# Dense expert weights built once per token over all 128 first keys, with one-hots laid out by pairs of tokens and a contiguous stationary operand

## Chip, cores and metric

One core of a Trainium2 chip runs the whole program. The metric is device time in microseconds (us), median over runs. The engines named below are PE (matrix multiply; PEld is its weight load), DVE (vector), ACT (scalar), POOL and SP (in this part only issuers of DMAs). Every engine runs its own instructions in program order and waits on semaphores for the others.

## What is computed

The program is two transformer layers of different kinds; the change lies in the feed-forward part of the first, a product-key mixture with 16,384 tiny experts (`peer_ffn`), for 256 tokens:

```python
q = (h @ w_q).reshape(b, s, PEER_HEADS, 2, PEER_HALF)
sc = jnp.einsum('bshpc,hpkc->bshpk', q, sub_keys)
top_v, top_i = lax.top_k(sc, PEER_TOPK)                # 16 of 128 keys, twice per head
cand_i = top_i[..., 0, :, None] * PEER_KEYS + top_i[..., 1, None, :]
best_v, best_pos = lax.top_k(cand_v, PEER_TOPK)        # 16 of 256 pairs per head
idx = jnp.take_along_axis(cand_i, best_pos, axis=-1)   # 8 heads x 16 experts per token
gate = jax.nn.softmax(best_v, axis=-1)
act = jax.nn.gelu(jnp.einsum('chkd,cd->chk', u_tab[idx], h))
out = jnp.einsum('chk,chkd->cd', gate * act, v_tab[idx])
```

An expert's number is (first key) x 128 + (second key). The reference gathers 128 experts per token; the kernel computes all 16,384 densely.

## The kernel before

The experts are a 128 x 128 grid: second key on the partitions, first key along the free axis. `act[0]` and `act[1]` are two tiles of 128 partitions x 64 first keys x 256 tokens (f32), one for each half of the first keys. Three kinds of work make the part:

- `u_phase(half)` (L1245) computes gelu(U h) for one half. It goes by pairs of first keys. A pair is one PSUM tile `pa` of 512 columns, and each of its two keys needs one 512 KB item of the weight stream and 24 matmuls of 256 columns (the weights are split into a high and a low part, and three products are added). It yields after the first key and after the second, so 64 steps in all. ACT applies the gelu from PSUM into `act[half]` (L1253).
- `g_phase(half)` (L1274) makes the dense routing weights G of one half and multiplies them into `act[half]`. It goes by groups of 8 tokens, 32 groups. `prep` makes on DVE three things in f16: `b`, the one-hot of the first keys (64 keys x 8 tokens, L1279); `a`, the one-hot of the second keys (128 x 8, L1281); and `c`, which is `b` times the gate in a high and a low part (two multiplies, L1283). The partition here is the token's 128 chosen experts. For each of the 8 tokens two matmuls follow, stationary `a[:, :, i]` and moving `c[:, q, :, i]` of 64 columns, both with neighbouring elements 8 halves apart. A DVE instruction (L1297) multiplies the PSUM tile into `act[half]`. A group is two steps, `prep` of the next group and the matmuls.
- `v_phase(half)` (L1314) multiplies the result with the V table: per first key one stream item and 12 matmuls of 512 columns, accumulated over both halves in four PSUM banks (`vacc`, tiles `pb`). Per two keys `split_to` (L386) splits `act` into a high part on ACT and a low part on DVE.

Order and overlap are written out by hand: `weave(main, (side, rate))` (L268) takes `rate` steps of the side generator after each step of the main one. Engines get their instructions in that order. Before: `u_phase(0)` with the routing; then `u_phase(1)` with G of half 0 (rate 1.05); then `v_phase(0)` with G of half 1 (rate 1.04); then `v_phase(1)`. Below these stages are called U0, U1, V0 and V1.

Weights arrive as f32 through a `Stream` (L140): SP issues a 512 KB load, ACT writes the high part (L200), DVE the low part (L211). `take` (L257) hands out an item; in it, DVE first gets the low part of the item that was split at the `take` before, then ACT gets the split of a further item if a slot is free. In these stages there are three slots for split items. So the low part for item j+2 stands in DVE's order just ahead of item j+1's other work, and PE wants it when it comes to item j+2.

PSUM has eight banks of 512 f32 columns: four for `pa`, four for `pb`. The tiles `xt` and `misc` lend their space for the one-hots; `xt` is put by in DRAM (`x1d`) and loaded again by a POOL DMA (L1348).

Of the kernel before, what the change touches and what calls it, by code (L numbers as in the profile page):

```python
# [7 lines left out]
F32 = mybir.dt.float32  # L8
FR = mybir.dt.float32r
BF = mybir.dt.bfloat16  # L10
HF = mybir.dt.float16
I32 = mybir.dt.int32
U32 = mybir.dt.uint32
AF = mybir.ActivationFunctionType
OP = mybir.AluOpType
AX = mybir.AxisListType
PSUM = bass.MemoryType.PSUM
# [250 lines left out]
def weave(main, *sides):  # L268

    sides = [[s[0], s[1], s[2] if len(s) > 2 else 0, 0.0] for s in sides]  # L270
    for n, _ in enumerate(main):
        for s in sides:
            if n < s[2]:
                continue
            s[3] += s[1]
            while s[3] >= 1.0 and s[0] is not None:
                s[3] -= 1.0
                if next(s[0], "end") == "end":
                    s[0] = None
# [21 lines left out]
def run(g):  # L301
    for _ in g:
        pass
# [13 lines left out]
def program(ctx, tc, A, out, dbg=None, stop=None, force=False):  # L317
    nc = tc.nc
    V, T, G, E = nc.vector, nc.scalar, nc.gpsimd, nc.tensor

    def dump(name, ap):
        if dbg is not None and name in dbg:
            nc.gpsimd.dma_start(dbg[name], ap)
# [5 lines left out]
    def pool(stack, name, bufs=1, side=None):  # L329
        kw = {} if side is None else {"side": side}  # L330
        return stack.enter_context(tc.tile_pool(name=name, bufs=bufs, reuse_waits="tile", **kw))

    const = pool(ctx, "const")
    strm = pool(ctx, "strm")
    psum = ctx.enter_context(tc.tile_pool(name="psum", bufs=4, space=PSUM))
    resid = pool(ctx, "resid")
    small = pool(ctx, "small", 3)
    x1d = ctx.enter_context(tc.tile_pool(name="dram", bufs=1, space=bass.MemoryType.DRAM)).tile([128, 2, D], F32, name="x1d")
# [11 lines left out]
    def pa():  # L350
        return psum.tile([128, 512], F32, name="pa")

    def pb():
        return psum.tile([128, 512], F32, name="pb")

    def load_const(p, name, eng=None):
        t = p.tile(list(A["c_" + name].shape), F32, name="c_" + name)
        (eng or nc.gpsimd).dma_start(t, A["c_" + name])
        return t
# [5 lines left out]
    def mm(p, a, b, s, e):  # L365
        E.matmul(p, a, b, start=s, stop=e)  # L366
# [23 lines left out]
    def flat(ap):  # L390
        return ap.rearrange("p a b -> p (a b)")
# [13 lines left out]
    def fm_tile(p, blk, nk, xh, xl, first=False):  # L405
        if first:

            b = [blk() for _ in range(nk)]
            for i, (w, x) in enumerate(((0, xh), (0, xl), (1, xh))):
                for k in range(nk):  # L410
                    mm(p, b[k][w], x[:, k], i + k == 0, i == 2 and k == nk - 1)
            return
        for k in range(nk):
            h, l = blk()
            mm_fm(p, h, l, xh[:, k], xl[:, k], k == 0, k == nk - 1)
# [48 lines left out]
    def halves(held, one, after):  # L464
        for t in range(2):
            for n in range(2):
                for i, (h, l, f) in enumerate(held):
                    one(t, n, i, h, l)
                    if t and n:
                        st.free_hl(f)  # L470
                    if i == 1:
                        yield
                after(t, n)
                yield

    xt = resid.tile([128, 2, D], F32, name="xt")
# [12 lines left out]
    misc = pool(phr, "pmisc", side="right").tile([128, 2048], F32, name="misc")  # L489
# [333 lines left out]
    for m in range(NF):  # L823
        st.add("ffn", A["w_ffn"], 3 * m, 3 * m + 2)
        if m >= LAG:
            q = m - LAG
# [30 lines left out]
    with Pools() as pha:  # L857
# [43 lines left out]
        iota = load_const(const, "iota")  # L901
# [139 lines left out]
        def acc1(n):  # L1041
            return lambda: [[(pb()[:, :n], 0, n)] for t in range(2)]
# [20 lines left out]
        for h in range(6):  # L1063
            heads.append(dict(q=qk[:, h], k=qk[:, 6 + h // 3], v=(lambda kt, h=h: va[:, kt, (h // 3) * 128:(h // 3) * 128 + 128]),
                              base=0, d=128, first=True, last=True, i=h, finish=fin(0), mode="win",
                              scale=128.0 ** -0.5, mask=wmask, sinkb=sinkb))
# [59 lines left out]
    ph1, ph0 = Pools(), Pools()  # L1126
    ctx.push(lambda *e: ph1.close())
    ctx.push(lambda *e: ph0.close())
    act = [None, pool(ph1, "pR", side="right").tile([128, 64, 256], F32, name="act1")]
# [4 lines left out]
    keys = act[1][:, 16:24].rearrange("p a (b c) -> p (a b) c", b=2)  # L1134
# [41 lines left out]
    def routing():  # L1176
        V.tensor_copy(io16, iota[:, :16, None].to_broadcast([128, 16, 16]))
        for tt in range(2):
# [63 lines left out]
    weave(lin_fm("pq", range(0, 16, 2), XH, XL, lambda m, p: T.activation(flat(qf[:, m:m + 2]), p, AF.Copy)),  # L1242
          (rt, 2.7, 8))

    def u_phase(half):  # L1245
        blk = Blocks("u")
        for k in range(0, 64, 2):
            p = pa()
            for i in range(2):
                fm_tile(p[:, i * 256:i * 256 + 256], blk, 8, XH, XL)  # L1250
                if i == 0:
                    yield
            T.activation(flat(act[half][:, k:k + 2]), p, AF.Gelu_apprx_tanh)  # L1253
            yield

    weave(u_phase(0), (rt, 2.7))
# [1 line left out]
    dump("idT", idT)  # L1258


    io8 = misc[:, 768:1280].bitcast(HF).rearrange("p (a b) -> p a b", b=8)
    ib = misc[:, 1280:1536].bitcast(HF).rearrange("p (a b) -> p a b", a=2)
    gp = misc[:, 1536:1792].bitcast(HF).rearrange("p (a b) -> p a b", a=2)
    V.tensor_copy(io8, iota[:, :, None].to_broadcast([128, 128, 8]))
    V.tensor_copy(ib, idT[:, 0:2])
    V.tensor_scalar(idT[:, 2], idT[:, 2], 32768.0, None, op0=OP.mult)
    V.tensor_copy(gp[:, 0], idT[:, 2])
    V.tensor_sub(gp[:, 1], idT[:, 2], gp[:, 0])

    oha = [xt[:, 0, i * 512:i * 512 + 512].bitcast(HF).rearrange("p (k t) -> p k t", t=8) for i in range(2)]  # L1270
    ohc = [ap.bitcast(HF).rearrange("p (q k t) -> p q k t", q=2, t=8) for ap in (xt[:, 1, 0:512], misc[:, 0:512])]
    ohb = [xt[:, 1, i:i + 256].bitcast(HF).rearrange("p (k t) -> p k t", t=8) for i in (512, 768)]

    def g_phase(half):  # L1274

        def prep(n):
            t = slice(n * 8, n * 8 + 8)
            a, b, c = oha[n % 2], ohb[n % 2], ohc[n % 2]
            V.tensor_tensor(b, io8[:, half * 64:half * 64 + 64], ib[:, 0, None, t].to_broadcast([128, 64, 8]),  # L1279
                            op=OP.is_equal)  # L1280
            V.tensor_tensor(a, io8, ib[:, 1, None, t].to_broadcast([128, 128, 8]), op=OP.is_equal)  # L1281
            for i in range(2):
                V.tensor_tensor(c[:, i], b, gp[:, i, None, t].to_broadcast([128, 64, 8]), op=OP.mult)  # L1283

        prep(0)
        yield
        for n in range(32):
            if n < 31:
                prep(n + 1)
                yield  # L1290
            a, c = oha[n % 2], ohc[n % 2]
            p = pa()
            for i in range(8):
                for q in range(2):
                    mm(p[:, i * 64:i * 64 + 64], a[:, :, i], c[:, q, :, i], q == 0, q == 1)
            v = act[half][:, :, n * 8:n * 8 + 8]
            V.scalar_tensor_tensor(v, p.rearrange("p (t k) -> p k t", t=8), 2.0 ** -15, v, op0=OP.mult, op1=OP.mult)  # L1297
            yield

    vacc = []  # L1300
# [1 line left out]
    def v_parts(half):  # L1302

        done = set()

        def need(k):
            for q in (k, k + 1):
                if q < 32 and q not in done:
                    done.add(q)
                    s = (q % 4) * 2  # L1310
                    split_to(YH[:, s:s + 2], YL[:, s:s + 2], act[half][:, q * 2:q * 2 + 2])
        return need

    def v_phase(half, R, after):  # L1314
        need = v_parts(half)

        def part(X):
            def f(k):
                need(k // 2)
                return X[:, k % 8]  # L1320
            return f
        if half == 0:
            vacc.extend([[pb(), pb()] for _ in range(2)])
        for k in range(64 - R):
            need(k // 2)
            h, l = st.take("vt")
            for t in range(2):
                v_mm(half, k, t, h, l)
            yield
        if R:  # L1330
            held = [st.keep("vt") for _ in range(R)]
            for k in range(64 - R, 64):
                need(k // 2)
            yield from halves(held, lambda t, n, i, h, l: v_mm(half, 64 - R + i, t, h, l, (n,)), after)

    def v_mm(half, k, t, h, l, ns=(0, 1)):
        ts = slice(t * 128, t * 128 + 128)
        for n in ns:
            mm_tm(vacc[t][n], h[:, HS[n]], l[:, HS[n]], YH[:, k % 8, ts], YL[:, k % 8, ts],
                  half == 0 and k == 0, half == 1 and k == 63)  # L1340

    g0, g1 = g_phase(0), g_phase(1)
    weave(u_phase(1), (g0, 1.05))
    run(g0)
    dump("act0", act[0])
    weave(v_phase(0, 0, None), (g1, 1.04))
    run(g1)
    nc.gpsimd.dma_start(xt, x1d)  # L1348
    ph0.close()

    st.extend(pool(ctx, "strmc"), 2, 1, len(st.items), "c")
# [55 lines left out]
    pg = pool(phx, "pg", side="right")  # L1407
# [40 lines left out]
    with Pools() as ph:  # L1448
# [40 lines left out]
        for h in range(12):  # L1489
            b = (h % 2) * 64  # L1490
            heads.append(dict(q=qs[b:b + 64, h // 2], k=kap(h // 4, b),
                              v=(lambda kt, h=h: vs[:, kt, (h // 4) * 64:(h // 4) * 64 + 64]), base=b, d=64,
# [17 lines left out]
    with Pools() as ph:  # L1510
# [10 lines left out]
        for m in range(NF):  # L1521
            p = pa()
# [20 lines left out]
    with Pools() as ph:  # L1543
# [70 lines left out]
        for h in range(12):  # L1614
            b = (h % 2) * 64
            heads.append(dict(q=qf[b:b + 64, h // 2], k=qf[b:b + 64, 6 + h // 2],
                              v=(lambda kt, h=h: vf[:, kt, h * 64:h * 64 + 64]), base=b, d=64,
# [121 lines left out]
    with Pools() as ph:  # L1739
# [186 lines left out]
        for n in range(NE * 11):  # L1926
            e, j = divmod(n, 11)
# [23 lines left out]
        e, yp = NE - 1, yps.pop(NE - 1)  # L1951
        gBe, bBe = st.spare(), st.spare()
        ln_load(3, gBe, bBe)
        a = turn(last)
# [6 lines left out]
        b = [small.tile([128, 2, 6], F32, name="bn") for _ in range(2)]  # L1961
# [34 lines left out]
```

## Time and profile before

| | |
|---|---|
| Median of three runs (lowest) | 2499.32 us (2498.3) |
| The profiled execution's own time | 2496.38 us |
| Its span, first to last instruction | 2494.6 us |
| Granted PE clock over the span | 0.993 |
| PE busy / DVE busy / ACT busy | 98% / 75% / 56% |

The stages follow each other without a common barrier. U0 ends at about 547 us (with the routing beside it from about 330), U1 runs from there to about 787, V0 to about 1028, V1 to about 1210. A view by windows gives busy time per engine in a stretch; a view of lines gives groups of equal instructions with their mean time; a timeline gives starts. Where instructions on one engine overlap in the records, the distance of their starts is what one costs in a row, and it can be shorter than the recorded duration.

### The profile page before, as it was taken

How to read it: one execution, taken by the hardware profiler on the slowest of the kernel's cores; microseconds unless marked ns; L12 is line 12 of the kernel's file. 1: busy time of each engine (PE TensorE's matmuls, PEld its weight loads, DVE VectorE, ACT ScalarE, POOL GpSimd, SP SyncE). 2: the span in 40 equal slices, each digit the busy share in tenths (PEclk: the TensorE clock that was granted, in tenths of full speed). 3: DMA queues.
4: the chain of work that ended last, by engine and by line, in shares of the span. 5: the costliest groups of instructions: out<-in, count | busy, mean ns of one | idle time of the engine just before them, and what ended most of it. 6: DMA issues, size and time to landing. Idle time of an engine off the chain costs nothing. (4 is left out here: it accounts for less than half of the span.)

```text
span 2494.6 us, 38669 instructions
## 1 busy us (share of the span) xinstructions
PE 2439.9 (98%) x14776; PEld 2125.6 (85%) x14776; DVE 1880.2 (75%) x2923; ACT 1393.0 (56%) x1859; POOL 35.2 (1%) x48
## 2 busy tenths in 40 slices
PE   9999999999999999999999999989899999999997
PEld 8888999999999888788868998768788888888885
DVE  7776669886666666665677548579889999999997
ACT  5775444443333333454544444438677877877775
POOL 0100000000000000000000000000000000000000
PEclk9999999999999999999999999989999999999999
DMA  7345555554444444756524554359899999999992
GB/s 266 117 132 181 186 178 180 175 173 133 143 136 141 139 135 143 254 187 190 174 93 178 186 195 146 121 217 336 307 340 346 368 341 344 366 355 338 363 357 89
DMA packets 149652, 545.62 MB, mean 219 GB/s; under 512 B 16960, under 2 KB 17088, under 8 KB 148816
## 3 DMA queue, kind: packets, MB, share of 16 engines
q1 hardware_dynamic: 145728, 528.55, 61.5%
q0 software_dynamic: 2720, 10.50, 1.3%
q10 hardware_dynamic: 1008, 4.00, 0.4%
q8 instruction: 118, 1.93, 0.3%
q14 instruction: 78, 0.64, 0.1%
HBM read 540.88 MB, written 2.10 MB: 218 GB/s over the span
## 5 line engine op out<-in xcount | busy, mean ns | idle before, releaser
L200 ACT ACTIVATE hwb<-rawb 128x1024 fp32r<-128x1024 f32 (+1 forms) x406 | 428.5, 1057 | 333.6 <-PE pa L366 132.5
L211 DVE TENSOR_TENSOR lwb<-rawb,hwb 128x1024 fp32r<-128x1024 f32 (+1 forms) x406 | 493.5, 1224 | 77.0 <-ACT hwb L200 75.1
L366 PE MATMUL pa<-XH,hwb 128*128 128x256 f32 x1848 | 509.1, 283 | 0.4 <-ACT XH L502 0.3
L366 PE MATMUL pa<-XH,lwb 128*128 128x256 f32 x1848 | 501.8, 280 | 2.7 <-DVE lwb L211 2.6
L366 PE MATMUL pa<-XL,hwb 128*128 128x256 f32 x1848 | 500.9, 279 | 0.0
L366 PEld LDWEIGHTS pa<-XH,hwb 128*128 128x128 f32 x1848 | 341.6, 188 | 4.4 <-issue 1.3
L366 PEld LDWEIGHTS pa<-XH,lwb 128*128 128x128 f32 x1848 | 340.2, 188 | 5.1 <-DVE lwb L211 4.9
L366 PEld LDWEIGHTS pa<-XL,hwb 128*128 128x128 f32 x1848 | 340.5, 188 | 1.1
L211 DVE TENSOR_TENSOR lwb<-rawe,hwb 128x1024 fp32r<-128x1024 f32 x176 | 210.9, 1222 | 23.9 <-ACT hwb L200 19.0
L200 ACT ACTIVATE hwb<-rawe 128x1024 fp32r<-128x1024 f32 x176 | 185.7, 1058 | 25.5 <-PE pb L366 11.6
L211 DVE TENSOR_TENSOR lwb<-rawf,hwb 128x1024 fp32r<-128x1024 f32 x130 | 156.6, 1222 | 17.8 <-ACT hwb L200 13.0
L1297 DVE SCALAR_TENSOR_TENSOR act<-pa,act 128x512 f32<-128x512 f32 x64 | 44.3, 692 | 164.2 <-PE pa L366 164.2
L366 PE MATMUL pb<-hwb,XH 128*128 128x512 f32 (+1 forms) x428 | 166.5, 389 | 1.2 <-ACT XH L387 1.2
L366 PE MATMUL pb<-hwb,XL 128*128 128x512 f32 (+1 forms) x428 | 165.5, 387 | 0.0
L366 PE MATMUL pb<-lwb,XH 128*128 128x512 f32 (+1 forms) x428 | 164.9, 385 | 0.0
L366 PE MATMUL pa<-hwb,XH 128*128 128x512 f32 x396 | 159.0, 401 | 0.0
L366 PE MATMUL pa<-hwb,XL 128*128 128x512 f32 x396 | 156.8, 396 | 0.0
L366 PE MATMUL pa<-lwb,XH 128*128 128x512 f32 x396 | 156.2, 395 | 0.0
L200 ACT ACTIVATE hwb<-rawf 128x1024 fp32r<-128x1024 f32 x130 | 137.1, 1059 | 23.2 <-PE pa L366 11.4
L366 PEld LDWEIGHTS <-xt 128*128 128x128 f16 x1024 | 119.9, 147 | 10.3 <-issue 8.9
L1253 ACT ACTIVATE act<-pa 128x512 f32<-128x512 f32 x64 | 38.3, 599 | 156.1 <-PE pa L366 156.1
L366 PE MATMUL pb<-hwb,aH 128*128 128x512 f32 x264 | 104.5, 396 | 0.0
(606 smaller groups left out, 5172.0 us busy)
## 6 DMA issues: line engine op xcount, KB each, us to landing
rawe<-w_e SPq DMA_DIRECT2D x220, 512.0 KB, 5.2
rawf<-w_e SPq DMA_DIRECT2D x152, 512.0 KB, 5.2
rawb<-w_u SPq DMA_DIRECT2D x128, 512.0 KB, 3.6
rawb<-w_e SPq DMA_DIRECT2D x112, 512.0 KB, 5.3
rawb<-w_vt SPq DMA_DIRECT2D x110, 512.0 KB, 3.6
rawb<-w_ffn SPq DMA_DIRECT2D x47, 512.0 KB, 4.4
rawc<-w_e SPq DMA_DIRECT2D x44, 512.0 KB, 5.1
rawb<-w_mrg SPq DMA_DIRECT2D x36, 512.0 KB, 3.7
```

Source lines behind the costliest of these rows:

```text
L200: self.nc.scalar.activation(h[:, :n], r[:, :n], AF.Copy)
L211: self.nc.vector.tensor_sub(l[:, :n], r[:, :n], h[:, :n].bitcast(F32))
L366: E.matmul(p, a, b, start=s, stop=e)
L1253: T.activation(flat(act[half][:, k:k + 2]), p, AF.Gelu_apprx_tanh)
L1297: V.scalar_tensor_tensor(v, p.rearrange("p (t k) -> p k t", t=8), 2.0 ** -15, v, op0=OP.mult, op1=OP.mult)
```

## The change

- There is one `g_phase` over all 128 first keys, woven into U1 at rate 1.56; V0 has no side work.
- A group is still 8 tokens, and a token now needs two matmuls of 128 columns instead of two times two of 64. PSUM tile `pg` has 1024 columns, two banks, and there are two of them. They take the place of the four `pb` banks during U1, through pools that are closed and opened again.
- The one-hots are laid out as 4 pairs of tokens x 128 keys x 2 tokens. `c` (high and low) keeps this layout, so the moving operand's neighbours are 2 halves apart. The one-hot of the second keys is made in `oh2` and then copied by ACT into `a`, a row of 128 neighbouring halves per token, the stationary operand. `prep` is now two steps (two equality tests and the copy; two multiplies), so a group is three steps.
- G for a half-1 key that U1 hasn't reached is written to `act[1]` by ACT with the scale. Then `u_phase` applies gelu in place in PSUM for the tokens whose G is there, gelu into `act[1]` for the others, and DVE multiplies the PSUM part into `act[1]`. For keys that are already done, DVE multiplies G into `act` as before.
- The reload of `xt` is issued ahead of V0 instead of behind it.

```diff
+    def psum_b(n, name):
+        bank_b.close()
+        return bank_b.enter_context(tc.tile_pool(name=name, bufs=n, space=PSUM))
+    psb = [psum_b(4, "psb")]
...
     def pb():
-        return psum.tile([128, 512], F32, name="pb")
+        return psb[0].tile([128, 512], F32, name="pb")
...
+    seen = {"k": 0, "t": 0}
     def u_phase(half):
...
-            T.activation(flat(act[half][:, k:k + 2]), p, AF.Gelu_apprx_tanh)
+            n, pv, to = seen["t"], p.rearrange("p (k t) -> p k t", k=2), act[half][:, k:k + 2]
+            if n == 0:
+                T.activation(to, pv, AF.Gelu_apprx_tanh)
+            else:
+                T.activation(pv[:, :, :n], pv[:, :, :n], AF.Gelu_apprx_tanh)
+                if n < 256:
+                    T.activation(to[:, :, n:], pv[:, :, n:], AF.Gelu_apprx_tanh)
+                V.tensor_mul(to[:, :, :n], pv[:, :, :n], to[:, :, :n])
+            seen["k"] += 2
...
+    oha = [xt[:, 0, i * 512:i * 512 + 512].bitcast(HF).rearrange("p (t k) -> p t k", t=8) for i in range(2)]
+    oh2 = misc[:, 1024:1536].bitcast(HF).rearrange("p (u k j) -> p u k j", u=4, j=2)
+    ohc = [ap.bitcast(HF).rearrange("p (q u k j) -> p q u k j", q=2, u=4, j=2) for ap in (xt[:, 1], misc[:, 0:1024])]
-    def g_phase(half):
+    def g_phase(ps):
         def prep(n):
...
+            def pairs(x, i):
+                return x[:, i, n * 8:n * 8 + 8].rearrange("p (u j) -> p u j", j=2)[:, :, None].to_broadcast([128, 4, 128, 2])
+            keys = io2[:, None].to_broadcast([128, 4, 128, 2])
+            V.tensor_tensor(c[:, 0], keys, pairs(ib, 0), op=OP.is_equal)
+            V.tensor_tensor(oh2, keys, pairs(ib, 1), op=OP.is_equal)
+            T.activation(a.rearrange("p (u j) k -> p u j k", j=2), oh2.rearrange("p u k j -> p u j k"), AF.Copy)
+            yield
+            for i in (1, 0):
+                V.tensor_tensor(c[:, i], c[:, 0], pairs(gp, i), op=OP.mult)
+            yield
...
-                    mm(p[:, i * 64:i * 64 + 64], a[:, :, i], c[:, q, :, i], q == 0, q == 1)
-            v = act[half][:, :, n * 8:n * 8 + 8]
-            V.scalar_tensor_tensor(v, p.rearrange("p (t k) -> p k t", t=8), 2.0 ** -15, v, op0=OP.mult, op1=OP.mult)
+                    mm(p[:, i * 128:i * 128 + 128], a[:, i], c[:, q, u, :, j], q == 0, q == 1)
+            pv = p.rearrange("p (t k) -> p k t", t=8)
+            ts, K = slice(n * 8, n * 8 + 8), seen["k"]
+            for half in range(2):
+                lo, hi = half * 64, half * 64 + 64
+                m = min(max(K, lo), hi)
+                if m > lo:
+                    v = act[half][:, :m - lo, ts]
+                    V.scalar_tensor_tensor(v, pv[:, lo:m], 2.0 ** -15, v, op0=OP.mult, op1=OP.mult)
+                if m < hi:
+                    T.activation(act[half][:, m - lo:, ts], pv[:, m:hi], AF.Copy, scale=2.0 ** -15)
+            seen["t"] += 8
...
-    g0, g1 = g_phase(0), g_phase(1)
-    weave(u_phase(1), (g0, 1.05))
-    run(g0)
-    weave(v_phase(0, 0, None), (g1, 1.04))
-    run(g1)
+    g = g_phase(psum_b(2, "psg"))
+    weave(u_phase(1), (g, 1.56))
+    run(g)
+    psb[0] = psum_b(4, "psb2")
     nc.gpsimd.dma_start(xt, x1d)
+    run(v_phase(0, 0, None))
```

## Rows read from the trace of the kernel before

**Rows 1.** Busy time by stage (U0 later part, U1, V0, V1 inner part); columns as named.

```profile
core 0: us, PE busy (x) PEld busy (x) DVE busy (x) ACT busy (x) POOL busy (x), PEclk, DMA share, GB/s
360.00:548.00 188.00, 185.84 (x1570) 184.25 (x1570) 170.55 (x431) 90.89 (x105) 0.00 (x0) 1.00 0.58 177
548.00:790.00 242.00, 240.80 (x2024) 238.62 (x2023) 146.04 (x224) 83.60 (x97) 0.00 (x0) 1.00 0.45 140
790.00:1030.00 240.00, 240.00 (x1276) 201.53 (x1275) 164.84 (x257) 84.61 (x97) 4.23 (x8) 1.00 0.45 142
1040.00:1190.00 150.00, 148.58 (x641) 120.72 (x640) 91.07 (x100) 77.84 (x91) 0.00 (x0) 1.00 0.65 211
```

**Rows 2.** Timeline of PE around one G group in U1: start, us, instruction.

```profile
706.16 2.14 PE L366 MATMUL pa<-misc,xt 128*128 128x64 f16 x16
708.05 0.37 PE L366 MATMUL pa<-XH,hwb 128*128 128x256 f32 x1
```

**Rows 3.** Timeline of PE, end of U1 and start of V0; then inside V1.

```profile
785.76 0.28 PE L366 MATMUL pa<-XH,lwb 128*128 128x256 f32 x1
...
786.47 0.28 PE L366 MATMUL pa<-XH,lwb 128*128 128x256 f32 x1
787.95 0.50 PE L366 MATMUL pb<-hwb,XH 128*128 128x512 f32 x1 [1.20 <-ACT XH L387]
...
1119.69 0.39 PE L366 MATMUL pb<-hwb,XH 128*128 128x512 f32 x1
...
1120.62 0.39 PE L366 MATMUL pb<-lwc,XH 128*128 128x512 f32 x1
```

**Rows 4.** Weight loads of three kinds: count, duration in ns min/median/max.

```profile
L366 PEld LDWEIGHTS <-xt x1024: 141/146/175, 552.4 to 1023.8; 128*128 128x128 f16 x171
L366 PEld LDWEIGHTS <-qk x60: 95/98/147, 1.2 to 13.9; 128*128 128x128 bf16 x60
L366 PEld LDWEIGHTS pa<-XH,hwb x8: 187/188/190, 14.4 to 15.3; 128*128 128x128 f32 x8
```

**Rows 5.** DVE and ACT groups in U1: count, busy us, mean ns, idle before.

```profile
L211 DVE TENSOR_TENSOR lwb<-rawb,hwb 128x1024 fp32r<-128x1024 f32 x64 | 77.8, 1217 | 1.4 <-ACT hwb L200 1.4
L200 ACT ACTIVATE hwb<-rawb 128x1024 fp32r<-128x1024 f32 x63 | 66.7, 1059 | 59.0 <-PE pa L366 59.0
L1297 DVE SCALAR_TENSOR_TENSOR act<-pa,act 128x512 f32<-128x512 f32 x32 | 22.1, 692 | 90.5 <-PE pa L366 90.5
L1281 DVE TENSOR_TENSOR xt<-misc 128x1024 f16<-128x1024 f16 x31 | 21.2, 685 | 0.0
L1253 ACT ACTIVATE act<-pa 128x512 f32<-128x512 f32 x32 | 19.2, 600 | 99.4 <-PE pa L366 99.4
```

**Rows 6.** Routing's DVE work on 2-byte and 4-byte tiles: ns min/median/max, or mean.

```profile
L1226 DVE TENSOR_TENSOR act<-act x8: 1205/1221/1231, 407.2 to 534.6; 128x1024 bf16<-128x1024 bf16 x8
L1198 DVE TENSOR_TENSOR act<-act x16: 403/416/423, 376.3 to 505.4; 128x256 f32<-128x256 f32 x16
L1229 DVE TENSOR_REDUCE act<-act 128x64 f32<-128x1024 bf16 x8 | 18.2, 2270 | 0.1
L1222 DVE TENSOR_TENSOR act<-act x8: 673/684/697, 406.5 to 532.9; 128x1024 bf16<-128x1024 bf16 x8
```

**Rows 7.** Timeline of DVE in U1: start, us, instruction, idle before.

```profile
627.82 0.69 DVE L1297 SCALAR_TENSOR_TENSOR act<-pa,act 128x512 f32<-128x512 f32 x1 [3.05 <-PE pa L366]
628.42 1.22 DVE L211 TENSOR_TENSOR lwb<-rawb,hwb 128x1024 fp32r<-128x1024 f32 x1
629.56 0.42 DVE L1279 TENSOR_TENSOR xt<-misc 128x512 f16<-128x512 f16 x1
629.89 0.69 DVE L1281 TENSOR_TENSOR xt<-misc 128x1024 f16<-128x1024 f16 x1
630.49 0.76 DVE L1283 TENSOR_TENSOR xt<-xt,misc 128x512 f16<-128x512 f16 x2
```

**Rows 8.** An ACT instruction out of PSUM with 384 elements: ns min/median/max.

```profile
L1237 ACT ACTIVATE misc<-pa x2: 486/489/492, 440.2 to 543.8; 128x384 f32<-128x384 f32 x2
```

More of the change, by code (lines that the diff above doesn't have):

```diff
@@ L335, in program @@
     psum = ctx.enter_context(tc.tile_pool(name="psum", bufs=4, space=PSUM))
+    bank_b = Pools()
+    ctx.push(lambda *e: bank_b.close())
+    def psum_b(n, name):
+        bank_b.close()
+        return bank_b.enter_context(tc.tile_pool(name=name, bufs=n, space=PSUM))
+    psb = [psum_b(4, "psb")]
     resid = pool(ctx, "resid")
@@ L1258, in program @@
     dump("idT", idT)
[L1261 to L1264, printed above, removed]
+    poh = pool(ph1, "poh", side="right").tile([128, 384], F32, name="ohk")
+    io2 = poh[:, 0:128].bitcast(HF).rearrange("p (a b) -> p a b", b=2)
+    ib = poh[:, 128:384].bitcast(HF).rearrange("p (a b) -> p a b", a=2)
+    gp = misc[:, 1792:2048].bitcast(HF).rearrange("p (a b) -> p a b", a=2)
+    V.tensor_copy(io2, iota[:, :, None].to_broadcast([128, 128, 2]))
     V.tensor_copy(ib, idT[:, 0:2])
@@ L1268, in program @@
     V.tensor_sub(gp[:, 1], idT[:, 2], gp[:, 0])
-    oha = [xt[:, 0, i * 512:i * 512 + 512].bitcast(HF).rearrange("p (k t) -> p k t", t=8) for i in range(2)]
-    ohc = [ap.bitcast(HF).rearrange("p (q k t) -> p q k t", q=2, t=8) for ap in (xt[:, 1, 0:512], misc[:, 0:512])]
-    ohb = [xt[:, 1, i:i + 256].bitcast(HF).rearrange("p (k t) -> p k t", t=8) for i in (512, 768)]
-    def g_phase(half):
+    oha = [xt[:, 0, i * 512:i * 512 + 512].bitcast(HF).rearrange("p (t k) -> p t k", t=8) for i in range(2)]
@@ L1276, in prep @@
+    oh2 = misc[:, 1024:1536].bitcast(HF).rearrange("p (u k j) -> p u k j", u=4, j=2)
+    ohc = [ap.bitcast(HF).rearrange("p (q u k j) -> p q u k j", q=2, u=4, j=2) for ap in (xt[:, 1], misc[:, 0:1024])]
+    def g_phase(ps):
         def prep(n):
[L1277 to L1286, printed above, removed]
+            a, c = oha[n % 2], ohc[n % 2]
+            def pairs(x, i):
+                return x[:, i, n * 8:n * 8 + 8].rearrange("p (u j) -> p u j", j=2)[:, :, None].to_broadcast([128, 4, 128, 2])
+            keys = io2[:, None].to_broadcast([128, 4, 128, 2])
@@ L1287, in g_phase @@
+            V.tensor_tensor(c[:, 0], keys, pairs(ib, 0), op=OP.is_equal)
[5 more added lines that the diff above has]
+            yield
+        yield from prep(0)
         for n in range(32):
             if n < 31:
-                prep(n + 1)
@@ L1290, in g_phase @@
-                yield
+                yield from prep(n + 1)
             a, c = oha[n % 2], ohc[n % 2]
-            p = pa()
+            p = ps.tile([128, 1024], F32, name="pg")
             for i in range(8):
+                u, j = i // 2, i % 2
                 for q in range(2):
-                    mm(p[:, i * 64:i * 64 + 64], a[:, :, i], c[:, q, :, i], q == 0, q == 1)
-            v = act[half][:, :, n * 8:n * 8 + 8]
-            V.scalar_tensor_tensor(v, p.rearrange("p (t k) -> p k t", t=8), 2.0 ** -15, v, op0=OP.mult, op1=OP.mult)
+                    mm(p[:, i * 128:i * 128 + 128], a[:, i], c[:, q, u, :, j], q == 0, q == 1)
```

## The prediction

> **What bounds the kernel now.** I read the busy time by stage first, since the change touches two stages only. In U1 PE is busy for 240.8 of 242.0 us, in V0 for 240.0 of 240.0, at a granted clock of 1.00; DVE has 146 and 165, ACT 84 and 85 [rows 1]. DVE's multiply of G waits for PE in every group, about 3 us each time [rows 5, 7]. So both stages are bound by PE, and the reader should count PE time alone, as long as DVE and ACT keep room.
>
> Then the PE timeline gives prices as distances of starts, since recorded matmul durations overlap. Sixteen G matmuls stand between 706.16 and 708.05: 1.89 us, 0.118 each [rows 2]. A 256-column matmul of the U kind costs (786.47 - 785.76)/6 = 0.118, a 512-column one (1120.62 - 1119.69)/4 = 0.232 [rows 3]. The difference, 0.114 for 256 columns, says that streaming 128 columns takes 0.057 us; 64 would take 0.029. The old G matmul pays 0.118 for 64 columns, so columns aren't what it pays for.
>
> **V0.** All of g1 leaves this stage: 32 groups x 1.89 = 60.5 us of PE time [rows 2], in a stage in which PE has no gap [rows 1]. What remains is 768 matmuls at 0.232, 178 us. Can the rest of the chain feed that? The inner part of V1 is the same loop without G: 148.58 us busy in 150 [rows 1]; U0 runs PE at 185.84 of 188 with the same three slots and items of 2.8 us, although DVE is busy for 170 of it with the routing. In V0 ACT and DVE lose or keep work. **Term: -60.5 us.**
>
> **U1, PE.** The 32 groups stay, with as many matmuls as before, 512, now of 128 columns. Below they cost 0.057 (streaming alone), above 0.118 (as now). Between these, the weight loads decide: the G load with elements 8 halves apart takes 146 ns, one of 128 neighbouring halves 98, one of f32 187 [rows 4]. The new stationary operand is the middle kind, and the moving one goes from 8 halves apart to 2. An f32 load that takes 187 keeps up with one matmul per 118 in U1; one that takes 98 is about 90 shorter and should keep up with anything that streaming allows. I take 0.065, near the lower end: 512 x 0.065 = 33.3 against 60.5. **Term: -27.2 us** (bounds -31.3 and 0).
>
> [...]
>
> **U1, DVE.** Per group, four instructions of 128x1024 f16 take the place of one such and three of 128x512. [...] Nearest rows: a three-level pattern with 16 neighbours, broadcast in the middle, takes 684 ns for 1024; with the broadcast innermost 1221; a strided reduction over 2-byte elements 2270 [rows 6]. An operand that repeats one 4-byte word 16 times took 416 for 256, no more than 1.04 ns an element plus some 0.15 fixed [rows 6], and here the operand that repeats does so by one 4-byte word. Innermost step is 1, as in the first row, so I take 685: 4 x 32 x 0.685 = 87.7.
>
> The rest of DVE's U1: low parts 64 x 1.217 = 77.9; half-0 multiply 32 x 0.692 = 22.1 [rows 5]. For half 1 I counted the woven order: 32 multiplies of G with 8,448 elements in all, and 30 tensor products with 7,936. At the same 0.15 + 0.00105 per element that is 13.6 and 12.8. Sum 214 us. In a row each costs some 0.08 less than recorded (628.42 to 629.56 is 1.14 for 1.22; 629.89 to 630.49 is 0.60 for 0.69 [rows 7]); 286 instructions make 190 us. PE's U1 is 64 items x 24 x 0.118 = 181, plus 33: 214. DVE keeps 24 us of room, but its waits must fit in.
>
> **U1, waits.** I walked one pair of keys (Ua, Ub) by the issue order. Most common: L211; [Ua] multiplies of prep; L211; [Ub] tensor product; G multiplies; equality tests; next L211. With Ub's matmuls starting at 0, they end at 2.8; ACT's gelu in PSUM needs 0.4 to 0.8 (0.60 for 512 elements, 0.49 for 384 [rows 5, 8]), so the product ends near 4.1; G's matmuls end at 3.9, so the G multiplies end near 5.1, the tests at 6.3, the low part at 7.4. PE reaches that item at 2.8 + 1.04 + 2.8 = 6.7 and wants the low part in its third matmul, 6.9. So PE stalls for 0.5 us. As 1.56 doesn't divide evenly, the order slides through six patterns; walked the same way, 20 of 32 pairs stall by 0.3 to 0.55 and the rest don't. **Term: +9**, with 0 and +25 (0.8 in each pair) as bounds. G's banks (two, a group apart 7 us) and `pa` (four, 5.6 us of matmuls each) come free in time.
>
> **ACT** has 67 for splits, 34 for the copies (32 x 1.06, as a 128x1024 split [rows 5]), 24 for gelu in two parts (61 instructions; 0.86 ns an element and 0.16 fixed from [rows 5, 8]), 12 for G's copies: 137 of 214 us, so nothing. If it read every second half twice as slowly, 34 more would still fit.
>
> **Edges.** At U1's end the last product (0.69) stands ahead of the first low split on DVE; PE idles 1.2 us there now [rows 3]: +1 at most. The earlier reload of `xt` is needed only at V1's end. The smaller setup of one-hot keys is hidden behind U1's first matmuls. Zero for these, +1 for the edge.
>
> **Sum:** -60.5 - 27.2 + 9 + 1 = -77.7. The profiled execution took 2496.4 (span 2494.6, about 1.8 around it): 2418.7. The median stands 2.9 above it: **2422 us**, 3.1% faster. Its own range, from the bounds of pace and stalls, is 2404 to 2440.
>
> **Rivals.**
> *The weight path stays at 0.118.* For it: f32 loads of neighbouring elements, 128 columns wide, don't go much faster, and the load could cost the same whatever its stride. Against: 98 ns against 146 [rows 4]. Then PE keeps 60.5 in U1, stalls of some 0.4 per pair add 13, and only V0 gains: -46.5, 2453.
>
> *One-hots by pairs lose the fast mode* (1221 [rows 6]): 128 x (1.221 - 0.685) = 69 more, DVE 259, and DVE bounds U1 at some 262 with its waits, 20 above now: -40, 2459. For it: no row has runs of two. Against: step 1 in the innermost place, as in the 684 row. [...]
>
> *Slower:* the pair layout costs as much as the strided reduction, 2270 [rows 6]. DVE's U1 becomes 190 + 128 x 1.585 = 393, 151 above the present 242; less 60.5: 2590. The point at which it decides: DVE above 242 + 60.5 = 302, which is 1.56 us per one-hot instruction. Against it: that row isn't a two-operand elementwise one, and all of those in the rows stay at 1221 or under.
>
> **Chances.** Forecast 0.70; weight path as before 0.11; no fast mode 0.12; slower 0.07. The second and third lie within 2% (50 us, about what a measurement of this kernel tells from no change), the second so near that I give a third of it to faster. Faster 0.74, same 0.19, slower 0.07. The range must hold the first two and most of the third: 2402 to 2460.
>
> **What would show it.** After the change V0 should last about 179 us with PE at 98% or more, and no f16 matmul in it. In U1, 512 f16 loads of about 98 ns, groups of 16 matmuls in 0.95 to 1.1 us (1.9 would be the second case); one-hot instructions at 685 (1221 the third); PE waits named by L211, 5 to 15 us in all; U1 some 225 us. Were U1's idle PE time above 30 us, my walk of the order would be wrong; were V0 above 185, the feeding of V0.

## The result, and the profile after

| | before | after |
|---|---|---|
| Median | 2498.81 us | 2427.68 us |
| Ratio, with its 95% interval | | 0.9718, 0.9702 to 0.9735 |
| The profiled execution, its span | 2496.38, 2494.6 | 2430.09, 2428.3 |

The change makes the kernel 2.8% faster. The forecast was 2422, its range 2402 to 2460. (One run of the kernel before, 4474.01 us, was disturbed and is left out of the ratio.)

The total is close, but its parts are not. To see that, set the first V0 matmul against the span. Before it stands at 787.95 [rows 3]; after, by the timeline of PE, here:

```profile
663.34 1.08 PE L375 MATMUL pg<-misc,xt 128*128 128x128 f16 x16
664.24 0.37 PE L375 MATMUL pa<-XH,hwb 128*128 128x256 f32 x1
...
784.52 0.50 PE L375 MATMUL pb<-hwb,XH 128*128 128x512 f32 x1 [1.20 <-ACT XH L396]
```

So U1 and all before it gave 3.4 us only, and everything from V0 on gave 2494.6 - 787.95 = 1706.7 against 2428.3 - 784.52 = 1643.8: 62.9. Yet the G matmuls in U1 did become cheap, 0.90 us for sixteen (663.34 to 664.24) against 1.89 [rows 2]: 32 x 0.99 = 31.7 us. About 28 of them were lost again. The busy time by stage says where to look (columns as in [rows 1]):

```profile
548.00:784.00 236.00, 218.38 (x2022) 210.49 (x2022) 193.90 (x285) 127.45 (x189) 0.54 (x1) 0.99 0.43 144
785.00:962.00 177.00, 176.94 (x767) 144.58 (x766) 97.70 (x97) 84.44 (x97) 4.77 (x9) 1.00 0.60 198
```

V0 is what it was meant to be: PE without a gap. In U1 PE is no longer always busy, 218 of 236, and DVE has gone from 146 of 242 [rows 1] to 194. The view of waits of U1 names them (who waited for whom: us in total, times, longest):

```profile
ACT act L1333 <- DVE act L1331: 60.9, 32, 3.0
DVE act L1273 <- ACT act L1272: 37.4, 29, 2.8
ACT xt L1308 <- DVE misc L1306: 36.4, 32, 2.9
...
PE pa L375 <- DVE lwb L211: 16.3, 22, 1.9
```

PE waits for low parts (L211). DVE itself waits in one place that matters: at the tensor product (L1273), for the gelu (L1272). ACT waits at G's copy (L1333) and at the one-hot copy (L1308). The wait of PE counts only idle time behind the modelled ends of matmuls. The distances of starts give the whole of it: from the first matmul of U1 to the first of V0, less the groups of G and less 1,536 matmuls of 256 columns at their plain pace of 0.118, 29.8 us are left over, where before it was 2.9.

The single prices came out as hoped: the groups of U1 by form (count, busy us, mean ns, idle before):

```profile
L211 DVE TENSOR_TENSOR lwb<-rawb,hwb 128x1024 fp32r<-128x1024 f32 x63 | 76.7, 1218 | 0.1
L1308 ACT ACTIVATE xt<-misc 128x1024 f16<-128x1024 f16 x32 | 33.9, 1058 | 36.4 <-DVE misc L1306 36.4
L375 PEld LDWEIGHTS <-xt 128*128 128x128 f16 x512 | 29.6, 97 | 1.4
L1311 DVE TENSOR_TENSOR misc<-misc 128x1024 f16<-128x1024 f16 x32 | 22.0, 688 | 0.6
L1306 DVE TENSOR_TENSOR misc<-ohk 128x1024 f16<-128x1024 f16 x32 | 21.9, 685 | 0.0
```

One-hots by pairs run at 685 ns, beside 684 and not 1221 [rows 6]; the loads at 97.

So two questions are left. Why does PE stall three times as long as the walk said? And what made a G matmul cost 0.12 us before?

### The profile page after: what moved, and what is told of

Its sections match the earlier page's. It is cut to its first block, busy times and chain, and to the rows that moved or that the text cites. A ratio compares the mean times of both kernels' runs of the same rounds, so it can differ in the third digit from the quotient of the medians.

```text
span 2428.3 us, 37627 instructions
## 1 busy us (share of the span) xinstructions
PE 2356.3 (97%) x14264; PEld 2042.7 (84%) x14264; DVE 1861.7 (77%) x2825; ACT 1438.0 (59%) x1952; POOL 35.2 (1%) x48
## 5 line engine op out<-in xcount | busy, mean ns | idle before, releaser
L211 DVE TENSOR_TENSOR lwb<-rawb,hwb 128x1024 fp32r<-128x1024 f32 (+1 forms) x406 | 493.9, 1225 | 91.2 <-ACT hwb L200 89.0
L375 PEld LDWEIGHTS pa<-XH,lwb 128*128 128x128 f32 x1848 | 340.7, 188 | 28.8 <-DVE lwb L211 28.3
L211 DVE TENSOR_TENSOR lwb<-rawe,hwb 128x1024 fp32r<-128x1024 f32 x176 | 210.9, 1222 | 24.3 <-ACT hwb L200 19.8
L200 ACT ACTIVATE hwb<-rawe 128x1024 fp32r<-128x1024 f32 x176 | 185.7, 1058 | 25.8 <-PE pb L375 11.9
L211 DVE TENSOR_TENSOR lwb<-rawf,hwb 128x1024 fp32r<-128x1024 f32 x130 | 156.6, 1223 | 17.8 <-ACT hwb L200 13.4
L200 ACT ACTIVATE hwb<-rawf 128x1024 fp32r<-128x1024 f32 x130 | 137.1, 1059 | 23.2 <-PE pa L375 11.4
L397 DVE TENSOR_TENSOR XL<-act,XH 128x512 fp32r<-128x512 f32 x64 | 44.1, 692 | 110.0 <-ACT XH L396 110.0
L375 PE MATMUL pb<-hwb,aL 128*128 128x512 f32 x264 | 104.2, 395 | 0.0
L375 PE MATMUL pb<-lwb,aH 128*128 128x512 f32 x264 | 104.2, 395 | 0.0
```

The costliest lines, as they stand in the source:

```text
L200: self.nc.scalar.activation(h[:, :n], r[:, :n], AF.Copy)
L211: self.nc.vector.tensor_sub(l[:, :n], r[:, :n], h[:, :n].bitcast(F32))
L397: V.tensor_sub(l, src, h.bitcast(F32))
```

## Experiments

The time of the kernel before beside these runs was 2497.7 to 2498.9 us; each row is a median.

| Run | What it is | Time, us | Ratio to before, 95% interval |
|---|---|---|---|
| after | the change | 2427.7 | 0.9718, 0.9702 to 0.9735 |
| e1_defer | product issued one key later | 2408.1 | 0.9641, 0.9625 to 0.9657 |
| e2_direct | no copy by ACT | 2421.9 | 0.9692, 0.9676 to 0.9709 |
| e5_defer_direct | both | 2410.1 | 0.9646, 0.9630 to 0.9662 |
| e8_defer_all | both, and G's multiplies later too | 2401.2 | 0.9612, 0.9596 to 0.9629 |
| e3_stat8 | stationary 8 halves apart, written by ACT | 2517.9 | 1.0075, 1.0059 to 1.0092 |
| e6_stat8_dve | the same, written by DVE | 2423.6 | 0.9704, 0.9688 to 0.9720 |
| e4_mov8 | moving 8 halves apart | 2514.4 | 1.0067, 1.0050 to 1.0084 |
| e7_before_pairs | kernel before, layout by pairs alone | 2410.8 | 0.9651, 0.9635 to 0.9667 |
| e9_before_movpairs | kernel before, moving by pairs alone | 2444.4 | 0.9779, 0.9762 to 0.9795 |

### Why PE stalls in U1

Three theories: the order of DVE's work (the product's wait has low parts queued behind it), DVE's load as such, and ACT's waits.

**The product one key later.** It is issued behind the next low part:

```diff
                 fm_tile(p[:, i * 256:i * 256 + 256], blk, 8, XH, XL)
                 if i == 0:
+                    call(pend); pend.clear()
                     yield
...
-                V.tensor_mul(to[:, :, :n], pv[:, :, :n], to[:, :, :n])
+                pend.append(lambda ...: V.tensor_mul(to[:, :, :n], pv[:, :, :n], to[:, :, :n]))
```

> The tensor product of a key pair is issued one key later, behind the next low part, instead of right after its gelu. In the changed kernel U1 takes some 240 us, PE's issue gaps there add up to 29 us, and DVE waits 37 us (29 times) for gelu at this product. Theory A, order: that wait, with low parts queued behind it, is what makes PE stall; then the wait at the product falls under 8 us, PE's gaps to 12 or less, and the time to 2405 to 2415 us. Theory B, load: DVE simply has too much work per key pair; then the gaps stay at 22 to 32 us with another wait in front of them, and the time at 2423 to 2431. Theory C, ACT: its waits (61 us at the copy of G, 36 at the one-hot copy) delay splits and gelu; then the time also stays at 2423 to 2431.

It took 2408.1. V0 starts at 764.69 in place of 784.52, and the waits of U1 have changed:

```profile
ACT act L1337 <- DVE act L1335: 52.1, 32, 2.5
ACT xt L1312 <- DVE misc L1310: 25.6, 24, 2.9
DVE act L1335 <- PE pg L375: 20.2, 25, 1.4
...
PE pa L375 <- DVE lwb L211: 4.7, 9, 1.0
...
764.69 0.50 PE L375 MATMUL pb<-hwb,XH 128*128 128x512 f32 x1 [1.20 <-ACT XH L396]
```

DVE's wait for gelu is gone from the list, PE's wait went from 16.3 to 4.7, and the extra distance of U1's matmuls from 29.8 to 11. DVE does the same work. So it is the order: theory A. ACT still waits 52 us at G's copy, and that costs nothing here.

**Without ACT's copy.** The stationary operand is read straight from the pair layout, neighbours 2 halves apart:

```diff
-            V.tensor_tensor(oh2, keys, pairs(ib, 1), op=OP.is_equal)
-            T.activation(a.rearrange(...), oh2.rearrange(...), AF.Copy)
+            V.tensor_tensor(a, keys, pairs(ib, 1), op=OP.is_equal)
...
-                    mm(p[...], a[:, i], c[:, q, u, :, j], q == 0, q == 1)
+                    mm(p[...], a[:, u, :, j], c[:, q, u, :, j], q == 0, q == 1)
```

> The copy of the one-hot by ACT is left out; the stationary operand is read from the pair layout, neighbours 2 halves apart. If only a distance of 16 bytes hurts a weight load, G matmuls stay at 0.058 to 0.065 us, loads at about 98 ns; ACT has 34 us less work and loses the 36 us wait. Then theory C wants 2410 to 2420 us, theories A and B 2423 to 2432. If the stationary row must be contiguous, the loads go to 120 to 146 ns, the pace to 0.09 to 0.12, and the time to 2435 to 2455.

2421.9, 5.8 less than the change, just below what theories A and B gave and above what C gave. PE doesn't miss the contiguous row at all, by form in U1 and what follows:

```profile
L375 PEld LDWEIGHTS <-xt 128*128 128x128 f16 x512 | 29.5, 97 | 1.3
L375 PE MATMUL pg<-misc,xt 128*128 128x128 f16 x256 | 17.6, 220 | 0.0
```

The same 97 ns and the same matmuls as after the change. The copy that gives each token a contiguous row brings nothing, and takes 34 us of ACT.

**Both.** The two edits above in one kernel.

> Both: the tensor product issued one key later, and the stationary operand read straight from the pair layout without ACT's copy. The first alone gave 2408.1 us, the second alone 2421.9, from 2427.7. If both act through the same wait for gelu (ACT's copy only made gelu later, and the product no longer waits for it), the second gives nothing more: 2406 to 2410. If ACT's copy also costs by itself, they add: 2400 to 2405.

2410.1, no better than the deferred product alone. So the copy cost its 5.8 us by making gelu later while DVE waited for it. The timeline of ACT shows where. After the change, in the pairs that start between 637 and 660 us, the copy and a split stand ahead of gelu (first two lines; the pair starts at 644.7). Without the copy (third line; the pair starts at 643.5) gelu of the same size comes 1.1 us earlier in its pair, and the stalls of these pairs go from 1.05 to 1.2 down to 0.4 to 0.7:

```profile
644.06 1.06 ACT L1308 ACTIVATE xt<-misc 128x1024 f16<-128x1024 f16 x1 [0.71 <-DVE misc L1306]
645.97 0.33 ACT L1270 ACTIVATE pa<-pa 128x208 f32<-128x208 f32 x1
...
643.67 0.33 ACT L1270 ACTIVATE pa<-pa 128x208 f32<-128x208 f32 x1 [0.44 <-PE pa L375]
```

ACT's waits are not a bound of their own: theory C falls.

**G's multiplies later as well**, by the same list, which is now called behind each item's matmuls:

```diff
-            pv = p.rearrange("p (t k) -> p k t", t=8)
-            ts, K = slice(n * 8, n * 8 + 8), seen["k"]
-            ...
+            def evac(n=n, pv=p.rearrange("p (t k) -> p k t", t=8)):
+                ts, K = slice(n * 8, n * 8 + 8), seen["k"]
+                ...
+            pend.append(evac)
```

> As the run with both edits, and the multiplies of G by DVE and ACT are issued behind the next low part as well. In the run with the deferred product alone, stalls of 0.7 to 1.0 us per key pair were left where multiplies of G or the product stand in a row ahead of a low part (11 us of gaps in U1). If they are due to the order, U1's gaps go to 3 to 6 us and the time to 2396 to 2402. If they are due to DVE's load, it stays within 2 us of the run with both edits.

2401.2, as the order asks and 9 us under the run with both edits. The stages and the start of V0:

```profile
548.00:757.00 209.00, 207.74 (x2007) 206.01 (x2005) 191.66 (x283) 96.46 (x157) 0.53 (x1) 1.00 0.49 163
758.00:934.00 176.00, 176.00 (x762) 143.99 (x763) 96.68 (x96) 83.43 (x96) 4.75 (x9) 1.00 0.60 195
...
757.03 0.50 PE L375 MATMUL pb<-hwb,XH 128*128 128x512 f32 x1 [1.21 <-ACT XH L396]
```

DVE is as busy as after the change (191.7 against 193.9), PE has 207.7 of 209.0, and U1 ends 27.5 us earlier. The extra distance of U1's matmuls is down to 4.6 us, near the 2.9 of before. Theory B, load, falls: DVE's load was never too large for U1, it stood in the wrong order.

### What an old G matmul paid for

The prediction said that the weight load decides. Each operand was put back by itself.

**Stationary 8 apart.** ACT writes the old distance into `a`:

```diff
-oha = [....rearrange("p (t k) -> p t k", t=8) ...]
+oha = [....rearrange("p (k u j) -> p u j k", u=4, j=2) ...]
...
```

> ACT writes the stationary one-hot with neighbours 8 halves apart, as before the change; the moving operand stays 2 apart. If the stationary side made the old 0.118 to 0.122 us per G matmul, the pace goes back to about 0.12 with loads of 146 ns, G costs PE 30 us more, and the time goes to 2440 to 2458 us (less than 30 more where PE's stalls take up part of it). If the moving side made it, the pace stays at 0.058 and the time at 2423 to 2432.

2517.9, far over both. But the groups by form, in U1 and what follows, show that the operand has little part in it:

```profile
L1308 ACT ACTIVATE xt<-misc 128x1024 f16<-128x1024 f16 x32 | 156.9, 4903 | 34.5 <-DVE misc L1306 34.5
...
L375 PEld LDWEIGHTS <-xt 128*128 128x128 f16 x512 | 36.2, 147 | 2.2 <-ACT xt L1308 0.7
```

The copy, 1058 ns after the change, takes 4903 when ACT writes with neighbours 8 halves apart, and ACT holds up the splits behind it: DVE's low parts wait 48 us for them, and PE is busy for 251 of U1's 326 us, at a granted clock of 0.92. The load has its old 147 ns, but the G matmuls' starts lie only 0.064 apart (median). The run says little by its time, so DVE was made to write that layout directly, with no copy:

```diff
...
-            V.tensor_tensor(oh2, keys, pairs(ib, 1), op=OP.is_equal)
-            T.activation(a.rearrange(...), oh2.rearrange(...), AF.Copy)
+            V.tensor_tensor(a, io2[:, :, None].to_broadcast([128, 128, 4, 2]), ..., op=OP.is_equal)
...
-                    mm(p[...], a[:, i], c[:, q, u, :, j], q == 0, q == 1)
+                    mm(p[...], a[:, :, u, j], c[:, q, u, :, j], q == 0, q == 1)
```

> DVE writes the second-key one-hot as 128 keys x 8 tokens and PE reads it there as the stationary operand, 8 halves apart, with no copy by ACT; the moving operand stays 2 apart. It mends the run in which ACT wrote that layout and took 4.9 us for each copy. If the stationary distance costs only what was seen there (pace 0.064 to 0.070 us, loads of 147 ns), G costs PE 3 to 6 us more than with neighbours 2 apart, and the time is 2421 to 2429 us. If it made the old pace, 0.12, the time is 2440 or more.

2423.6, beside 2421.9 with neighbours 2 apart. Sixteen matmuls take 655.06 to 656.10, 1.04 us or 0.065 each:

```profile
655.06 1.23 PE L375 MATMUL pg<-xt 128*128 128x128 f16 x16
656.10 0.36 PE L375 MATMUL pa<-XH,hwb 128*128 128x256 f32 x1
...
L375 PEld LDWEIGHTS <-xt 128*128 128x128 f16 x512 | 35.1, 147 | 1.4
```

**Moving 8 apart**, stationary contiguous:

```diff
-ohc = [....rearrange("p (q u k j) -> p q u k j", q=2, u=4, j=2) ...]
+ohc = [....rearrange("p (q k u j) -> p q k u j", q=2, u=4, j=2) ...]
...
-                    mm(p[...], a[:, i], c[:, q, u, :, j], q == 0, q == 1)
+                    mm(p[...], a[:, i], c[:, q, :, u, j], q == 0, q == 1)
```

> The first-key one-hot and its products are laid out as 128 keys x 8 tokens, so the moving operand's neighbours are 8 halves apart, as before the change; the stationary one stays contiguous. If the moving side made the old pace (64 columns in 0.118 to 0.122), 128 columns cost 0.12 to 0.24 us, G costs PE 30 to 90 us more and the time goes to 2445 to 2520 us. If only the stationary side counts, the pace stays at 0.058 to 0.065 and the time at 2423 to 2434. DVE's instructions have the same size and should stay at 685 ns.

2514.4. A group takes 652.42 to 655.84, 3.42 us or 0.214 a matmul, at a granted clock of 1.00 in that stretch:

```profile
652.42 3.79 PE L375 MATMUL pg<-xt 128*128 128x128 f16 x16
655.84 0.48 PE L375 MATMUL pa<-XH,hwb 128*128 128x256 f32 x1
...
652.40:655.80 3.40, 3.40 (x18) 1.74 (x17) 2.15 (x3) 1.76 (x2) 0.00 (x0) 1.00 0.05 13
```

That is 1.7 ns a column; the old 0.118 for 64 columns was 1.8. So the moving operand's distance made the old price. With it, half as many matmuls of twice the columns save little: 32 x 3.42 = 109 us against 64 x 1.89 = 121, and this run, the whole change but for that distance, comes out no faster than the kernel before (1.0067).

**Then the layout alone should do.** The kernel before, with nothing but pairs:

```diff
-ohc = [....rearrange("p (q k t) -> p q k t", q=2, t=8) ...]
+ohc = [....rearrange("p (q u k j) -> p q u k j", q=2, u=4, j=2) ...]
...
-                    mm(p[...], a[:, :, i], c[:, q, :, i], q == 0, q == 1)
+                    mm(p[...], a[:, u, :, j], c[:, q, u, :, j], q == 0, q == 1)
```

> The kernel before (G of one half in U1, of the other in V0, 1024 matmuls of 64 columns, no gelu in PSUM), with nothing changed but the layout: one-hots and products by pairs of tokens, both operands 2 halves apart, no copy. If the distance in the moving operand is what a G matmul paid for, 1024 of them go from 0.122 to between 0.029 (streaming alone) and 0.06 us, and the time falls by 60 to 95 us, to 2404 to 2438: as much as the whole change. If it was making G once per token that paid, the layout alone gives under 30 us: over 2468.

2410.8: 17 us better than the whole change, and the intervals lie apart. Sixteen 64-column matmuls take 0.50 us, 0.031 each, in U1 and V0 alike, and PE is full in both:

```profile
654.10 0.66 PE L366 MATMUL pa<-misc,xt 128*128 128x64 f16 x16
654.60 0.36 PE L366 MATMUL pa<-XH,hwb 128*128 128x256 f32 x1
...
548.00:743.00 195.00, 193.97 (x2005) 192.39 (x2003) 142.65 (x219) 81.84 (x95) 0.00 (x0) 1.00 0.56 172
744.00:940.00 196.00, 195.56 (x1274) 156.25 (x1275) 164.56 (x256) 83.63 (x96) 3.94 (x8) 1.00 0.55 171
```

1024 x 0.031 is 32 us, about what 512 matmuls of 128 columns cost after the change (32 x 0.90 = 29).

**The moving side alone**, stationary left 8 apart:

```diff
-                    mm(p[...], a[:, :, i], c[:, q, :, i], q == 0, q == 1)
+                    mm(p[...], a[:, :, u, j], c[:, q, u, :, j], q == 0, q == 1)
```

> The kernel before, with only the moving operand in pairs of tokens (2 halves apart); the stationary one stays 8 apart, 1024 matmuls of 64 columns. With both in pairs the pace is 0.030 us and the time 2410.8. If a load of 147 ns holds up a stream of 0.030 us matmuls by as much as it did at 128 columns (0.064 to 0.067), the pace is 0.06 to 0.07, G costs some 35 us more than with both, and the time is 2440 to 2452. If the load hides, the pace stays at 0.03 to 0.04 and the time at 2409 to 2422.

2444.4. Sixteen take 651.70 to 652.70, 0.0625 each:

```profile
651.70 1.16 PE L366 MATMUL pa<-misc,xt 128*128 128x64 f16 x16
652.70 0.36 PE L366 MATMUL pa<-XH,hwb 128*128 128x256 f32 x1
...
L366 PEld LDWEIGHTS <-xt 128*128 128x128 f16 x1024 | 67.6, 163 | 10.3 <-issue 8.9
```

So the two distances are separate floors: a load from 8 apart holds a matmul to about 0.06 us, at 64 columns (0.0625, e9) as at 128 (0.065, e6), and a moving operand from 8 apart to 1.7 to 1.8 ns a column. With 128 columns (0.057 of streaming) the first hardly shows, with 64 it costs 34 us (2444.4 - 2410.8). In the kernel before, the moving floor lay above the other and hid it: mending the moving side alone gave 54 us (2498.4 - 2444.4), and the stationary side then the 34.

## Why the prediction was right, and where not

**Rows and bound.** Right: both stages were PE's, and V0 without G is 177 us of PE without a gap.

**V0, -60.5.** Right in place and size: 62.9 from V0 on. But it was worth that only by the old layout. With pairs, V0 with its share of G lasts from 743.18 to the same point of V1 only some 20 us longer than without (197.8 against 177.9, by the 769th `pb` matmul). In the kernel before, it is 241.6. The prediction gave the whole term to making G once per token; e7 shows that the layout alone brings 44 of the 64 us between 241.6 and 177.9, and taking G out of V0 the other 20.

**U1, PE, -27.2.** The size was close: 0.90 us a group, 0.056 a matmul, the lower bound; 31.7. The reason was wrong. "Between these, the weight loads decide" is the step that failed, and with it "columns aren't what it pays for". The rows had both distances at 8 at once, and the argument from the load's 146 and 98 ns looked at one of them. A load from 8 apart gives 0.06 (e6, e9). The moving operand made the 0.12: by e4 its columns cost 1.7 ns each, and e9, which mends it alone, takes the old matmul from 0.118 to 0.0625. That the size came out all the same is luck: the change mended the moving side too. The rival in which the weight path stays at 0.118 fell with it. For its reason, that f32 loads 128 columns wide don't go much faster, the timeline of PE before has eight such matmuls in U0, from 331.81 to 332.62 (the lines below), 0.101 each. The f16 ones of the change cost 0.056. The moving operand cost 1.7 ns a column at a distance of 8 halves (e4) against 0.44 at 2 (0.90 us for 16 x 128 columns); no other distance was run for it, and only 1, 2 and 8 for the stationary one. What it is in a distance of 8 that costs isn't shown.

```profile
331.69 0.28 PE L366 MATMUL pa<-XH,lwb 128*128 128x256 f32 x1
331.81 1.05 PE L366 MATMUL pa<-act 128*128 128x128 f32 x8
332.62 0.36 PE L366 MATMUL pa<-XH,hwb 128*128 128x256 f32 x1
```

**U1, DVE.** Right: 685 to 688 ns for pairs, busy 194 us where 190 to 214 was worked out. The rival of the lost fast mode (1221 ns) fell, and so did the slower one (2270).

**U1, waits, +9.** This is the term that failed: 27, above its bound of 25 (29.8 - 2.9 by the distances of starts). U1 lasts 240 us instead of 225, and PE's wait for L211 is 16.3 where 5 to 15 was named. The 29.8 stay just under the 30 that was to tell of a wrong walk, though the walk was wrong. The mechanism was the one walked, as one late pair shows, by the timeline:

```profile
737.17 1.09 PE L375 MATMUL pg<-misc,xt 128*128 128x128 f16 x16
737.36 0.49 ACT L1270 ACTIVATE pa<-pa 128x400 f32<-128x400 f32 x1 [1.10 <-PE pa L375]
737.88 0.26 ACT L1272 ACTIVATE act<-pa 128x112 f32<-128x112 f32 x1
738.06 0.37 PE L375 MATMUL pa<-XH,hwb 128*128 128x256 f32 x1
738.18 0.57 DVE L1273 TENSOR_TENSOR act<-pa,act 128x400 f32<-128x400 f32 x1 [1.30 <-ACT act L1272]
738.67 1.18 DVE L1331 SCALAR_TENSOR_TENSOR act<-pg,act 128x512 f32<-128x512 f32 x2
739.77 0.68 DVE L1305 TENSOR_TENSOR misc<-ohk 128x1024 f16<-128x1024 f16 x1
740.37 0.69 DVE L1306 TENSOR_TENSOR misc<-ohk 128x1024 f16<-128x1024 f16 x1
740.97 1.22 DVE L211 TENSOR_TENSOR lwb<-rawb,hwb 128x1024 fp32r<-128x1024 f32 x1
...
742.24 0.39 PE L375 MATMUL pa<-XH,lwb 128*128 128x256 f32 x1 [0.87 <-DVE lwb L211]
```

Count from the end of the pair's matmuls (737.17). The walk had the product end after 1.3, G's multiplies after 2.3, the tests after 3.5, the low part after 4.6, and PE wanting it after 4.1. Measured: 1.5, 2.6, 3.8, 5.0 (PE goes on at 742.24), and PE would have gone on after 0.89 + 2.8 + 0.23 = 3.9. A stall of 1.1, not 0.5. Two things made it in this pair. The walk took the mean size for the product and for G's half-1 multiply (256 elements each), but both grow through U1, here to 400 and more, and a stall is cut off at zero, so its mean isn't the stall of the mean. And PE came 0.15 earlier than walked: what was gained on the G matmuls made the low part later by as much. Early pairs stall by 0.25 to 0.5, about as walked; 19 of the 32 stall by 0.85 or more (by the distances of starts, pair by pair). In such a late pair DVE, not PE, sets the pace: 6.4 us of work and 1.3 of waiting make the 7.7 us at which late pairs follow each other.

Size doesn't account for all 19. In eight of them, from 605 to 669 us, the product has 128 to 240 elements, less than the walk's mean, and they stall by 1.05 to 1.8; in three, from 710 to 730, it has 336 to 368, and they don't stall. So the walk had orders wrong too. From 605 to 637 both tests and both multiplies of `prep` stand between the product and the low part:

```profile
614.88 0.31 DVE L1273 TENSOR_TENSOR act<-pa,act 128x144 f32<-128x144 f32 x1 [1.82 <-ACT act L1272]
...
617.63 1.22 DVE L211 TENSOR_TENSOR lwb<-rawb,hwb 128x1024 fp32r<-128x1024 f32 x1
```

By the prediction's own prices that order makes the low part end after 1.3 + 4 x 0.6 + 1.1 = 4.8 where PE wants it after 4.1, a stall of 0.7 and not of 0.55. From 637 to 669 the copy makes gelu late (e2). And once, after PE had been idle from 671.96 to 673.86, the granted clock is 0.50 for some 3 us (675 to 677 and on). The 256-column matmuls stand 0.213 apart there in place of 0.118, so it costs about half of the 3 us, by an estimate from that stretch.

**Sum.** -62.9 - 31.7 + 28.3 = -66.3, the fall of the span, in place of -77.7. The 28.3 is what 31.7 leaves beside U1's 3.4; the stalls are 27 of it, and U1 starts 1.1 later. An error of +18 in the waits and edge and one of -7 in the matmuls went against each other. The spread of the runs hid half of the rest: the profiled execution before lay 2.4 under its median and the one after 2.4 above, so that the sum misses its own target by 11.4 (2418.7 against 2430.1) and the forecast the median by 5.7. That the total came so near is luck in part.

## What to carry to other kernels

When a small matmul costs more than its columns, ask for the distance between neighbours in both operands, and put one back at a time: here the moving one set the price and hid what the stationary one cost, and a layout by pairs of 2-byte elements mended both, with DVE's one-hots still at 685 ns (e7, 2410.8 from 2498). The restructuring around it first lost 17 us of that again. With its order mended (e8) it comes out 9.6 under the layout alone; the starts give 6 of that, U1 14 us longer and V0 20 shorter. On an in-order engine that also feeds the bound engine, issue whatever waits for a long chain (here matmul, gelu, product) behind the next piece of feed work: with no less work, that gave 20 us, and 27 with G's multiplies moved too and the copy gone. Walk such an order pattern by pattern, and with the sizes at both ends of a ramp, not with the mean.

The fastest version here is e8_defer_all, 2401.2 us, 0.9612 of before and 0.989 of the change (2401.2/2427.7).

## What the runs showed of the hardware that was not expected

- ACT writing 1024 f16 elements with neighbours 8 halves apart takes 4903 ns, against 1058 for rows of 128; DVE writes one-hots whose tokens are neighbours, and keeps 685 ns (e3, e6). ACT reading 2 apart cost nothing (1058, beside 1059 for a 128x1024 split [rows 5]).
- A moving operand with f16 neighbours 8 apart streams at 1.7 to 1.8 ns a column; 2 apart at 0.44 to 0.48 (0.056 for 128, 0.031 for 64), beside 0.45 to 0.46 for the f32 streams (0.232 for 512, 0.118 for 256 [rows 3]).
- A stationary one 2 apart loads as fast as a contiguous one, 97 ns both (e2, after); 8 apart it takes 147 (e6) to 163 (e9) and holds a matmul to about 0.06 us (0.065, 0.0625).
- In e4 the granted clock fell in U1, late in a group of G or just behind it. One group runs from 642.01 to 645.44; it begins at a granted clock of 1.00, the clock falls before it ends (0.69 from 644 to 646), and for some 3 us PE is at 0.50, though it is busy all the time; then it is back at 1.00. The group from 652.42 has 1.00 to 655.8, and from 656.16 the 256-column matmuls behind it stand the plain 0.118 apart; the one from 661.70 has 1.00 to 665.1, and from 665.53 those behind it stand 0.213 apart. U1 as a whole stood at 0.90 there, against 0.99 after the change, so e4's time holds a cost of the clock as well as that of the columns. What PE did ahead of the two falls was to stream 8 halves apart. In the kernel before it does so too, in groups of 1.89 us, and the clock stays at 1.00 in U1 and V0 [rows 1].

```profile
642.00:644.00 2.00, 2.00 (x11) 1.05 (x10) 1.97 (x3) 1.74 (x2) 0.00 (x0) 1.00 0.00 0
644.00:646.00 2.00, 2.00 (x10) 1.32 (x9) 0.33 (x2) 0.00 (x0) 0.00 (x0) 0.69 0.38 94
646.00:648.00 2.00, 2.00 (x12) 2.00 (x11) 1.89 (x3) 1.15 (x2) 0.00 (x0) 0.50 0.45 172
648.00:650.00 2.00, 2.00 (x18) 2.00 (x18) 0.00 (x0) 0.48 (x2) 0.00 (x0) 0.96 0.48 156
...
642.01 3.79 PE L375 MATMUL pg<-misc,xt 128*128 128x128 f16 x16
645.44 0.57 PE L375 MATMUL pa<-XH,hwb 128*128 128x256 f32 x1
```
